# A two-layer hybrid mixer on one core: the prologue put in the order in which tokens and modulation weights arrive

## The chip, the core and the metric

The kernel runs on one NeuronCore of one Trainium2 chip. Five engines have queues of their own, each worked off in order: TensorE (PE; its weight loads are listed apart as PEld), VectorE (DVE), ScalarE (ACT), GpSimd (POOL) and SyncE (SP, which here issues most of the DMA transfers). The metric is the time of one execution in microseconds, the median of several runs.

## What is computed

Two layers of a mixer on 1024 latent tokens and 256 context tokens, all of width 1024. The change touches only the beginning of the first layer:

```python
shift, scale, gate = jnp.split(jax.nn.silu(c) @ w_mod + b_mod, 3, axis=-1)
shift_c, scale_c, gate_c = jnp.split(jax.nn.silu(c_ctx) @ w_mod + b_mod, 3, axis=-1)
h = rms_norm(x, norm_g) * (1 + scale[:, None]) + shift[:, None]
hc = rms_norm(ctx, norm_g) * (1 + scale_c) + shift_c
...
p = h @ w_in
```

After that come Fourier mixing, pooling, attention, a gated output product and a residual, twice.

## The kernel before

A token tile is 128 tokens by 1024 channels. Tiles 0 to 3 are group 0, tiles 4 to 7 group 1 (both latent), tiles 8 and 9 group 2 (context). The channels are cut into eight slices k of 128. For each slice and group, here called a block (k, g), the prologue makes the transposed, modulated tokens `H[k]`, split into a high and a low part of 32-bit matmul operands, and multiplies them at once with the first gate chunk of `w_in`:

- a token tile is loaded by an SP transfer of 512 KB (`x_load`, L256); ScalarE squares it in two halves and sums (L266); GpSimd turns the sum into the factor 1/rms (L267 to L269, the last a power); VectorE scales the tile with it (`norm`, L575);
- TensorE transposes slice k of the tiles of the group into one PSUM bank (L280); VectorE (L286) or ScalarE (L284) applies scale and shift; ScalarE rounds to the high part (L287); GpSimd (groups 0 and 1) or VectorE (group 2) subtracts to get the low part (L289);
- TensorE does the block's gate product (`gk`, L340): six matmuls, two output halves times high by high, low by high and high by low, summed over k in PSUM.

Scale and shift come from `w_mod`. A modulation product q (0 to 3) reads four transfers of 512 KB (`mod0_load`, L148), and yields scale and shift of slices 2q and 2q+1. Products 0 to 2 are eight 32-bit matmuls on TensorE each (`mod0_mm`, L157), after which `mod0_fin` copies the row (VectorE, L162), transposes it back (TensorE, L166) and adds bias and gain (`mod_finish`, VectorE, L136 to L141). Product 3 is done by VectorE in 32 multiply-adds (L176, L178), and 16 small matmuls sum it (`mod0_sum`, L187).

SP issues in this order: twelve modulation transfers (products 0 to 2), two halves of the gate chunk, ten token tiles, four modulation transfers (product 3), the next weight chunk. The order of the blocks is written out by hand in `items`: slices 0 to 5 of group 0, then of group 1, then of group 2, then slices 6 and 7 of all three groups. The list `at` says at which place the norm of a tile and the pieces of product 3 are put in. The gate product of a block stands three blocks behind its transposes. PSUM has eight banks here; the six gate sums hold six of them.

After the prologue `fourier_mix` puts eight small matmuls (L384) into the TensorE queue, and the next chunk's product follows (L340 from 92.42 us on).

Of the kernel before, what the change touches and what calls it, by code (L numbers as in the profile page):

```python
# [31 lines left out]
def build(tc, I, out):  # L32
# [127 lines left out]
    def mod0_fin(q, pm):  # L160
        row = E2()
        dve.tensor_copy(row[0:2, :], pm[0:2, :])  # L162
# [4 lines left out]
        mod_finish(0, 2 * q, psv[:, 0], psv[:, 1])  # L167

    def mod0_acc(ws, acc):
        for k in range(KT):  # L170
            for i in range(2):
                w = ws[k // 2][:, k % 2, i * 256:i * 256 + 256]
                for t in range(2):
                    a, sk = acc[:, 2 * i + t, :], sc[:, k, t:t + 1]
                    if k == 0:
                        dve.tensor_scalar(a, w, sk, None, MULT)  # L176
                    else:
                        dve.scalar_tensor_tensor(a, w, sk, a, MULT, ADD)  # L178
            yield

    def mod0_sum(q, acc):
        ps = PX()
        psv = ps[:, 0:8].rearrange("p (i c t) -> p i c t", i=2, c=2)
        for i in range(2):
            for ct in range(2):
                for t in range(2):
                    pe.matmul(psv[:, i, ct, t:t + 1], lhsT=acc[:, 2 * i + t, ct * 128:ct * 128 + 128],  # L187
                              rhs=ones[:, 0:1], start=True, stop=True)
        mod_finish(0, 2 * q, psv[:, 0], psv[:, 1])
# [83 lines left out]
    def h_block(l, k, g, xn, H, on_act=False):  # L273
        tiles = GROUPS[g]
        s = 1 if g == 2 else 0
        n = 128 * len(tiles)
        c0 = tiles[0] * 128
        ps = PX()
        for i, j in enumerate(tiles):
            pe.transpose(ps[:, i * 128:i * 128 + 128], xn[j][:, k * 128:k * 128 + 128], ident)  # L280
# [8 lines left out]
        eng.tensor_tensor(H[k][1][:, c0:c0 + n], hf[:, :n], H[k][0][:, c0:c0 + n].bitcast(F32), SUB)  # L289

# [241 lines left out]
    def layer(l, src, dst, carry):  # L532
# [27 lines left out]
        if full:  # L560
# [16 lines left out]
            def hb(k, g, on_act):  # L577
                newH(k)
                h_block(l, k, g, xn, H, on_act)

            def gk(k, *gs):
                for ct in range(2):
                    proj_T_k(psg[ct], H, W, ct, ntokA, k, gs)
# [768 lines left out]
```

## Time and profile before

| | us |
|---|---|
| median of 3 runs | 1451.82 (1447.77 to 1453.87) |
| the profiled execution | 1448.99 |
| its span (first to last instruction) | 1447.0 |
| first gate matmul (TensorE, L340) | 38.14 |
| first matmul behind the prologue (L384) | 90.42 |
| first matmul of the next chunk's product (L340) | 92.42 |

The page gives for each engine the busy time and its share of the span. A row in order of time gives the start and the length in us, engine, line and operation, output and inputs, shape and count of what was merged, and in brackets how long the engine had been idle before it and what ended that. A stage row gives start and end of a stretch, its length, the busy us (and the count of instructions) of PE, PEld, DVE, ACT and POOL in that order, then the mean clock granted to TensorE as a share of 2.4 GHz (0.50 is 1.2 GHz), the busy share of the DMA engines and GB/s.

### The profile page before, as it was taken

The numbers are of one execution on the slowest core, as the hardware profiler recorded it, in microseconds if no ns is written. First come the engines' busy times: TensorE is split into PE (matmuls) and PEld (weight loads), VectorE is DVE, ScalarE is ACT, GpSimd is POOL, SyncE is SP. The second block draws the span as 40 slices with busy tenths as digits, with TensorE's granted clock in tenths as the row PEclk, the third lists the DMA queues.
The fourth block names the chain that finished last, engine by engine and source line by source line (L and its number), as shares of the span: only waits on it lengthen the run. The fifth ranks groups of instructions, "written<-read, shape, count | busy, mean of one in ns | idle before, by whom it ended". The sixth has DMA issues, their size and how long they took to land.

```text
span 1447.0 us, 24063 instructions
## 1 busy us (share of the span) xinstructions
PE 1381.8 (95%) x9364; PEld 1240.6 (86%) x9364; DVE 979.2 (68%) x1553; ACT 567.6 (39%) x1230; POOL 775.9 (54%) x827
## 2 busy tenths in 40 slices
PE   7899999899999998999999899999999999999998
PEld 1688899779999987888888778988999998888887
DVE  2853366886895178798898654573464319989896
ACT  2632212101232265666665433121131227656663
POOL 2543222456785057667677842226887107766664
PEclk9899999999999999999999999999999999999999
DMA  9220242575123032112113321526412202111110
GB/s 354 101 90 32 85 149 91 187 266 166 60 88 117 1 103 81 66 45 74 45 45 112 104 66 38 205 80 213 148 44 85 78 22 67 45 45 45 59 59 30
DMA packets 65153, 137.07 MB, mean 95 GB/s; under 512 B 7312, under 2 KB 19728, under 8 KB 65040
## 3 DMA queue, kind: packets, MB, share of 16 engines
q1 hardware_dynamic: 49712, 108.82, 22.5%
q10 hardware_dynamic: 15328, 26.72, 5.3%
q8 instruction: 74, 1.21, 0.3%
q14 instruction: 39, 0.32, 0.1%
HBM read 105.63 MB, written 29.88 MB: 94 GB/s over the span
## 4 chain that ended last, share of the span: by engine, by line
PE 46%; DVE 21%; POOL 7%; issue 3%; ACT 2%; DMA 2%; ACTq 0%; POOLq 0%; SPq 0%; DVEq 0%
PE x L360 16%; DVE sm L923 6%; PE S L913 6%; PE x L1056 6%; PE x L993 5%; PE x L340 5%; PE x L753 3%; DVE e L1020 3%; PE x L977 2%; DVE t L952 1%; DVE t L980 1%; POOL e L759 1%; POOL sm L803 1%; DVE t L210 1%; PE x L892 1%
## 5 line engine op out<-in xcount | busy, mean ns | idle before, releaser
L360 PE MATMUL x<-wh,t 128*128 128x256 f32 x2432 | 445.9, 285 | 0.1
L360 PEld LDWEIGHTS x<-wh,t 128*128 128x128 f32 x2432 | 381.7, 192 | 1.8 <-issue 1.0
L360 PE MATMUL x<-wl,t 128*128 128x256 f32 x1216 | 344.7, 283 | 0.0
L923 DVE TENSOR_REDUCE sm<-S 128x1 f32<-128x1280 f32 (+1 forms) x132 | 194.8, 1476 | 72.2 <-PE S L913 72.0
L360 PEld LDWEIGHTS x<-wl,t 128*128 128x128 f32 x1216 | 233.7, 192 | 1.3 <-issue 1.2
L913 PE MATMUL S<-t,e 128*128 128x512 f32 (+1 forms) x768 | 180.9, 371 | 2.8 <-ACT e L899 1.4
L340 PE MATMUL x<-t,wh 128*128 128x512 f32 (+1 forms) x640 | 173.3, 381 | 8.8 <-DVE t L289 4.3
L938 ACT ACTIVATE t<-S,sm 128x1280 f32<-128x1280 f32 (+1 forms) x140 | 171.7, 1230 | 1.2 <-DVE sm L923 1.2
L993 PE MATMUL x<-t,t 128*128 128x128 f32 x1312 | 157.5, 275 | 3.3 <-DVE t L980 2.7
L993 PEld LDWEIGHTS x<-t,t 128*128 128x128 f32 x1312 | 153.7, 192 | 6.4 <-DVE t L980 2.9
L913 PEld LDWEIGHTS S<-t,e 128*128 128x128 f32 x768 | 126.3, 190 | 20.6 <-ACT t L938 2.0
L340 PEld LDWEIGHTS x<-t,wh 128*128 128x128 f32 x640 | 114.1, 192 | 31.6 <-POOL t L289 5.4
L318 POOL TENSOR_TENSOR wl<-st,wh 128x1024 fp32r<-128x1024 f32 x36 | 93.1, 2587 | 84.3 <-ACT wh L317 83.6
L961 POOL TENSOR_TENSOR t<-t,t 128x768 f32<-128x768 f32 (+1 forms) x64 | 116.2, 1816 | 5.3
L317 ACT ACTIVATE wh<-st 128x1024 fp32r<-128x1024 f32 x64 | 64.8, 1059 | 138.4 <-DMA xpart<-e 45.8
L977 PE MATMUL x<-ident,t 128*128 128x128 f32 x636 | 101.2, 274 | 5.7 <-DVE e L1059 4.1
L953 POOL TENSOR_SCALAR t<-t,sm 128x768 f32<-128x768 f32 x62 | 83.4, 1344 | 42.8 <-DVE sm L949 26.6
L753 PE MATMUL x<-wh,t 128*128 128x512 f32 x288 | 93.6, 404 | 8.5 <-DVE t L528 4.7
L1056 PE MATMUL x<-wh,e 128*128 128x512 f32 (+1 forms) x312 | 98.9, 384 | 2.6 <-ACT e L899 1.0
L340 PE MATMUL x<-t,wl 128*128 128x512 f32 (+1 forms) x320 | 100.2, 374 | 0.0
L210 DVE SCALAR_TENSOR_TENSOR t<-t,sc,t 128x512 f32<-128x512 f32 x98 | 90.8, 968 | 1.5 <-DMA t<-in_wmB_dram 1.1
L977 PEld LDWEIGHTS x<-ident,t 128*128 128x128 f32 x636 | 75.1, 141 | 15.9 <-DVE e L1059 4.5
(224 smaller groups left out, 2318.0 us busy)
## 6 DMA issues: line engine op xcount, KB each, us to landing
st<-in_w_in_dram SPq DMA_DIRECT2D x48, 512.0 KB, 4.0
t<-in_wmB_dram ACTq DMA_DIRECT2D x24, 512.0 KB, 5.4
xpart<-e ACTq DMA_DIRECT2D x36, 256.0 KB, 3.8
t<-xpart SPq DMA_DIRECT2D x18, 512.0 KB, 3.9
t<-in_wmS_dram SPq DMA_DIRECT2D x16, 512.0 KB, 8.5
st<-in_w_out_dram SPq DMA_DIRECT2D x16, 512.0 KB, 5.1
t<-in_x_dram SPq DMA_DIRECT2D x10, 512.0 KB, 10.3
e<-in_x_dram SPq DMA_DIRECT2D x20, 256.0 KB, 4.5
```

The source lines that it names most:

```text
L210: dve.scalar_tensor_tensor(a, w, sk, a, MULT, ADD)
L318: lo_eng[hf].tensor_tensor(lo[:, sl, :], st, hi[:, sl, :].bitcast(F32), SUB)
L340: pe.matmul(p[:, :m], lhsT=W[wi][:, k, ct * 128:ct * 128 + 128], rhs=H[k][hi][:, c0:c0 + m], start=(n == 0), stop=(n == 3 * KT - 1))
L360: pe.matmul(bank[:, i * 256:i * 256 + 256], lhsT=H[k][hi][:, j * 128:j * 128 + 128], rhs=W[wi][:, k, :], start=(n == 0), stop=(n == 3 * KT ...
L753: pe.matmul(ps, lhsT=zr[k][zi][:, j * 128:j * 128 + 128], rhs=W[wi][:, k, :], start=(n == 0), stop=(n == 11))
L913: pe.matmul(S[:, i * nk + c:i * nk + c + n], lhsT=s["qT"][i][:, m * 2 + f, :], rhs=kT[2 * h + m][:, k0 + c:k0 + c + n], start=(f == 0), st ...
L923: dve.tensor_reduce(nb, S[:, :nh * nk].rearrange("p (h k) -> p h k", h=nh), AX.X, ALU.min)
L938: act.activation(p[:, sl], S[:, sl], AF.Exp, bias=nb[:, i:i + 1], scale=-1.0, accum_out=ls[:, i:i + 1])
L961: pool.tensor_tensor(p[0][:, cut:end], p[0][:, cut:end], p[1][:, cut:end], ADD)
L977: pe.transpose(ps[:, i * 128:i * 128 + 128], s["p"][0][:, (t0 + i) * 128:(t0 + i + 1) * 128], ident)
L993: pe.matmul(o[:, i * 128:i * 128 + 128], lhsT=s["PT"][:, i * nkt + t, :], rhs=vv[h][:, kt0 + t, :], start=(t == 0), stop=(t == nkt - 1))
L1056: pe.matmul(ps[:, :m], lhsT=zz[:, k, :], rhs=Wa[hf][wi][:, k, w0:w0 + m], start=(n == 0), stop=(n == 11))
```

## The change

SP now loads the gate chunk first, then tiles 0 to 3, modulation products 0 and 1, tiles 4 to 7, product 2, tiles 8 and 9, product 3, the next chunk. All four modulation products are matmuls on TensorE; they stand as entries 0 to 3 in `items`, among the blocks. `mod0_acc` and `mod0_sum` are gone, and the row's copy is now in `mod0_mm`. Of the factor 1/rms VectorE does the two small steps and GpSimd only the power. `h_block` is cut in two, `h_trans` (transposes) and `h_split` (the rest); at a modulation product the transposes of the next block are issued ahead of it. The six gate sums get their banks when they are first used. The line numbers of the same steps change: L157 to L155, L162 to L157, L166 to L164, L280 to L252, L284/L286 to L262/L264, L287 to L265, L289 to L267, L340 to L321, L575 to L561, L266 to L554, L269 to L557.

```diff
-    def mod0_mm(ws, half_way=None):
+    def mod0_mm(ws):
         ps = PX()
         for k in range(KT):
-            if k == KT // 2 and half_way:
-                half_way()
             pe.matmul(ps[0:2, :], lhsT=sc[:, k, :], rhs=ws[k // 2][:, k % 2, :], start=(k == 0), stop=(k == KT - 1))
-        return ps
...
         row = E2()
-        dve.tensor_copy(row[0:2, :], pm[0:2, :])
+        dve.tensor_copy(row[0:2, :], ps[0:2, :])
+        return row
...
-    def mod0_acc(ws, acc):
...
-    def mod0_sum(q, acc):
...
             def rms(*js):
                 for j in js:
                     rx[j] = SM(1)
-                    for _ in x_rms(xn[j], rx[j]):
-                        pass
+                    ss = SM(2)
+                    for hf in range(2):
+                        sq = E2()
+                        act.activation(sq, xn[j][:, hf * 512:hf * 512 + 512], AF.Square, accum_out=ss[:, hf:hf + 1])
+                    dve.tensor_tensor(rx[j], ss[:, 0:1], ss[:, 1:2], ADD)
+                    dve.tensor_scalar(rx[j], rx[j], 1.0 / D, EPS, MULT, ADD)
+                    pool.tensor_tensor(rx[j], rx[j], mhalf[:, 0:1], ALU.pow)
...
-            wm = [mod0_load(q) for q in range(3)]
             w_dma()
-            x_in(0, 1, 2, 3, 4, 5, 6, 7, 8, 9)
-            ms = [mod0_mm(wm[0])]
-            ms.append(mod0_mm(wm[1], lambda: mod0_fin(0, ms[0])))
-            ms.append(mod0_mm(wm[2], lambda: mod0_fin(1, ms[1])))
+            x_in(0, 1, 2, 3)
+            wm = [mod0_load(q) for q in range(2)]
+            x_in(4, 5, 6, 7)
+            wm.append(mod0_load(2))
+            x_in(8, 9)
+            wm.append(mod0_load(3))
             w_split()
             W = wready.pop(0)
...
-            items = [(k, g) for g in (0, 1, 2) for k in range(6)] + [(k, g) for k in (6, 7) for g in (0, 1, 2)]
+            w_dma()
+            for j in range(4):
+                rms(j)
+                norm(j)
+            items = [0, (0, 0), (1, 0), 1, (2, 0), (3, 0)] + [(k, 1) for k in range(4)] + [2]
+            items += [(k, g) for k in (4, 5) for g in (0, 1)] + [(k, 2) for k in range(6)] + [3]
+            items += [(k, g) for k in (6, 7) for g in (0, 1, 2)]
             at = {n: [] for n in range(len(items))}
...
+            for n, j in ((3, 4), (3, 5), (4, 6), (5, 7), (11, 8), (12, 9)):
+                at[n] += [lambda j=j: rms(j), lambda j=j: norm(j)]
+            late, ahead = [], {}
...
+            for n, it in enumerate(items):
+                if isinstance(it, int):
+                    look(n + 1)
+                    row = mod0_mm(wm[it])
                     for f in at[n]:
                         f()
-                    hb(*items[n], 6 <= n < 17)
...
+                    if late:
+                        gk(*late.pop(0))
+                    mod0_fin(it, row)
+                    continue
+                for f in at[n]:
+                    f()
+                newH(it[0])
+                look(n)
+                h_split(l, *it, ahead[it], H, n % 2 == 1 and n > 10)
+                late.append(it)
+                if len(late) > 3:
+                    gk(*late.pop(0))
...
                 if n == 22:
                     w_split()
                     w_dma()
+            for it in late:
+                gk(*it)
```

How the order of instructions changes is seen at three places. The first is VectorE where tiles 4 to 7 are scaled. Before, the scaling of a tile (L575, `t_21` to `t_24` are tiles 4 to 7) stands between the scale-and-shift steps (L286) of group 0:

```order
L286 TENSOR_SCALAR e_71_302<-x_297,scaleT_99,shiftT_97 128x512
L575 TENSOR_SCALAR t_21_158<-t_21_158,sm_286 128x1024
L286 TENSOR_SCALAR e_85_335<-x_330,scaleT_99,shiftT_97 128x512
L575 TENSOR_SCALAR t_22_160<-t_22_160,sm_319 128x1024
L286 TENSOR_SCALAR e_93_356<-x_351,scaleT_99,shiftT_97 128x512
L575 TENSOR_SCALAR t_23_162<-t_23_162,sm_340 128x1024
L286 TENSOR_SCALAR e_101_377<-x_372,scaleT_99,shiftT_97 128x512
L575 TENSOR_SCALAR t_24_164<-t_24_164,sm_361 128x1024
```

In the changed kernel, on VectorE, tiles 4 to 7 are `t_17` to `t_20`, and `x_276` is the sum of modulation product 1:

```order
L157 COPY e_65_285<-x_276 2x512
L555 TENSOR_TENSOR sm_287<-sm_288 128x1
L556 TENSOR_SCALAR sm_287<-sm_287 128x1
L561 TENSOR_SCALAR t_17_150<-t_17_150,sm_287 128x1024
L555 TENSOR_TENSOR sm_297<-sm_298 128x1
L556 TENSOR_SCALAR sm_297<-sm_297 128x1
L561 TENSOR_SCALAR t_18_152<-t_18_152,sm_297 128x1024
L136 TENSOR_TENSOR shiftT_97<-x_315,bmodT 128x4
```

The scaling of the four tiles now stands behind the copy of product 1's row.

The second place is ScalarE, where tiles 4 and 5 (`t_21`, `t_22`) were squared; before, the two squares of a tile stood there one tile at a time among the high parts (L287) of group 0:

```order
L266 ACTIVATE e_66_288,sm_287<-t_21_158 128x512
L266 ACTIVATE e_67_290,sm_287<-t_21_158 128x512
L287 ACTIVATE t_68_295<-e_71_302 128x512
L266 ACTIVATE e_80_321,sm_320<-t_22_160 128x512
L266 ACTIVATE e_81_323,sm_320<-t_22_160 128x512
L287 ACTIVATE t_82_328<-e_85_335 128x512
```

In the changed kernel ScalarE has this where tiles 6 (`t_19`) and 7 (`t_20`) are squared; `t_82` is the high part of block (2, 0), made from `e_84`, which VectorE writes behind the scaling of tile 6:

```order
L554 ACTIVATE e_80_327,sm_326<-t_19_154 128x512
L554 ACTIVATE e_81_329,sm_326<-t_19_154 128x512
L265 ACTIVATE t_82_335<-e_84_337 128x512
L554 ACTIVATE e_87_343,sm_342<-t_20_156 128x512
L554 ACTIVATE e_88_345,sm_342<-t_20_156 128x512
L265 ACTIVATE t_89_351<-e_92_358 128x512
```

The squares of tile 7 moved behind the high part of block (2, 0), whose scale and shift come from modulation product 1.

The third place is TensorE ahead of the first transposes of group 1 (`x_442`); before, the end of the gate product of block (2, 0) stood directly in front of them:

```order
L340 MATMUL x_231<-t_90_349,wh_221 128x512
L340 MATMUL x_231<-t_91_350,wh_221 128x512
L340 MATMUL x_231<-t_90_349,wl_222 128x512
L280 MATMUL x_442<-ident,t_21_158 128x128
L280 MATMUL x_442<-ident,t_22_160 128x128
L280 MATMUL x_442<-ident,t_23_162 128x128
L280 MATMUL x_442<-ident,t_24_164 128x128
```

In the changed kernel TensorE has this behind modulation product 1; the first row transposes its row back, `x_353` takes the transposes of block (3, 0), `x_362` those of (0, 1), and the last rows begin the gate product of (1, 0):

```order
L164 MATMUL x_315<-ident,e_65_285 128x2 x4
L252 MATMUL x_353<-ident,t_5_126 128x128
L252 MATMUL x_353<-ident,t_6_128 128x128
L252 MATMUL x_353<-ident,t_7_130 128x128
L252 MATMUL x_353<-ident,t_8_132 128x128
L252 MATMUL x_362<-ident,t_17_150 128x128
L252 MATMUL x_362<-ident,t_18_152 128x128
L252 MATMUL x_362<-ident,t_19_154 128x128
L252 MATMUL x_362<-ident,t_20_156 128x128
L321 MATMUL x_307<-t_59_260,wh_178 128x512
L321 MATMUL x_307<-t_60_261,wh_178 128x512
```

The transposes of group 1 moved from behind three gate products of group 0 to a place behind one; those of (1, 0), (2, 0) and (3, 0) now stand behind them.

## Rows read from the trace of the kernel before

**Rows 1.** The page, part 1: busy us, share of the span, instructions
```profile
PE 1381.8 (95%) x9364; PEld 1240.6 (86%) x9364; DVE 979.2 (68%) x1553; ACT 567.6 (39%) x1230; POOL 775.9 (54%) x827
```

**Rows 2.** Stages: start:end length, busy by engine (instructions), PEclk, DMA, GB/s
```profile
29.70:33.26 3.56, 0.34 (x5) 0.32 (x5) 2.09 (x3) 2.55 (x8) 3.13 (x9) 1.00 1.03 412
33.26:40.70 7.44, 6.16 (x23) 4.84 (x22) 4.96 (x10) 3.60 (x10) 5.30 (x10) 0.56 1.04 393
...
64.75:69.05 4.30, 1.20 (x8) 1.00 (x8) 4.30 (x13) 1.66 (x4) 0.00 (x0) 0.91 0.15 36
69.05:78.35 9.30, 9.30 (x44) 9.17 (x44) 6.38 (x18) 1.32 (x3) 0.14 (x1) 0.50 0.49 147
...
92.42:200.00 107.58, 107.58 (x622) 94.06 (x623) 45.77 (x81) 27.91 (x52) 29.50 (x18) 1.00 0.20 72
```

**Rows 3.** Order of time, ScalarE: start, length, engine, line, operation, [idle before <-releaser]
```profile
23.20 1.06 ACT L317 ACTIVATE wh<-st 128x1024 fp32r<-128x1024 f32 x1 [20.25 <-DMA st<-in_w_in_dram]
...
25.75 0.63 ACT L266 ACTIVATE e<-t 128x512 f32<-128x512 f32 x1 [0.23 <-DMA t<-in_x_dram]
```

**Rows 4.** Order of time, TensorE, 0 to 40 us
```profile
5.93 12.61 PE L157 MATMUL x<-t,sc 128*2 128x512 f32 x24 [5.93 <-DMA t<-in_wmS_dram]
...
18.80 7.03 PE L157 MATMUL x<-t,sc 128*2 128x512 f32 x16
25.76 0.40 PE L166 MATMUL x<-ident,e 2*128 2x2 f32 x4
...
38.14 1.50 PE L340 MATMUL x<-t,wh 128*128 128x512 f32 x2
```

**Rows 5.** Order of time, TensorE, end of the prologue
```profile
90.42 1.06 PE L384 MATMUL x<-e 128*128 128x128 f32 x8
```

**Rows 6.** Order of time, TensorE, one block of a latent group
```profile
56.11 0.71 PE L340 MATMUL x<-t,wh 128*128 128x512 f32 x2
...
57.58 0.60 PE L280 MATMUL x<-ident,t 128*128 128x128 f32 x4
57.94 0.72 PE L340 MATMUL x<-t,wh 128*128 128x512 f32 x2
```

**Rows 7.** Order of time, TensorE, one block of the context group
```profile
79.25 0.38 PE L280 MATMUL x<-ident,t 128*128 128x128 f32 x2
79.38 0.48 PE L340 MATMUL x<-t,wh 128*128 128x256 f32 x2
...
80.18 0.38 PE L280 MATMUL x<-ident,t 128*128 128x128 f32 x2
```

**Rows 8.** Order of time, VectorE, first and last step of one mod_finish
```profile
18.91 0.16 DVE L136 TENSOR_TENSOR shiftT<-x,bmodT 128x4 f32<-128x4 f32 x1 [3.09 <-PE x L166]
...
19.38 0.16 DVE L141 TENSOR_TENSOR scaleT<-sm,ngT 128x4 f32<-128x4 f32 x1
```

**Rows 9.** Instructions of one line, 0 to 95 us: count, ns min/median/max
```profile
L162 DVE COPY e<-x x3: 672/679/679, 15.1 to 32.2; 2x512 f32<-2x512 f32 x3
...
L575 DVE TENSOR_SCALAR t<-t,sm x10: 739/754/1768, 30.1 to 51.4; 128x1024 f32<-128x1024 f32 x10
...
L266 ACT ACTIVATE e<-t x20: 612/616/632, 25.8 to 49.3; 128x512 f32<-128x512 f32 x20
...
L269 POOL TENSOR_TENSOR sm<-sm,mhalf x10: 548/550/937, 29.5 to 50.8; 128x1 f32<-128x1 f32 x10
...
L286 DVE TENSOR_SCALAR e<-x,scaleT,shiftT x13: 528/800/811, 36.0 to 87.1; 128x512 f32<-128x512 f32 x10, 128x256 f32<-128x256 f32 x3
...
L289 POOL TENSOR_TENSOR t<-e,t x16: 1272/1314/1748, 37.5 to 84.8; 128x512 fp32r<-128x512 f32 x16
```

**Rows 10.** Groups, 0 to 92.5 us: count, busy us, mean ns, idle
```profile
L287 ACT ACTIVATE t<-e 128x512 fp32r<-128x512 f32 x16 | 10.1, 629 | 16.0 <-DVE e L286 15.7
...
L318 POOL TENSOR_TENSOR wl<-st,wh 128x1024 fp32r<-128x1024 f32 x2 | 5.6, 2802 | 25.2 <-ACT wh L317 25.2
...
L317 ACT ACTIVATE wh<-st 128x1024 fp32r<-128x1024 f32 x4 | 4.1, 1049 | 20.5 <-DMA st<-in_w_in_dram 20.5
```

More of the change, by code (lines that the diff above doesn't have):

```diff
@@ L150, in mod0_load, with mod0_fin @@
         return ws
-    def mod0_mm(ws, half_way=None):
+    def mod0_mm(ws):
         ps = PX()
         for k in range(KT):
-            if k == KT // 2 and half_way:
-                half_way()
             pe.matmul(ps[0:2, :], lhsT=sc[:, k, :], rhs=ws[k // 2][:, k % 2, :], start=(k == 0), stop=(k == KT - 1))
-        return ps
-    def mod0_fin(q, pm):
         row = E2()
-        dve.tensor_copy(row[0:2, :], pm[0:2, :])
+        dve.tensor_copy(row[0:2, :], ps[0:2, :])
+        return row
+    def mod0_fin(q, row):
         ps = PX()
@@ L166, in mod0_fin @@
             pe.transpose(ps[:, 2 * i:2 * i + 2], row[0:2, i * 128:i * 128 + 128], ident[0:2, 0:2])
-        mod_finish(0, 2 * q, psv[:, 0], psv[:, 1])
-    def mod0_acc(ws, acc):
[L170 to L179, printed above, removed]
-    def mod0_sum(q, acc):
[L182 to L188, printed above, removed]
         mod_finish(0, 2 * q, psv[:, 0], psv[:, 1])
@@ L271, in build, with h_trans, h_split @@
     GROUPS = {0: (0, 1, 2, 3), 1: (4, 5, 6, 7), 2: (8, 9)}
-    def h_block(l, k, g, xn, H, on_act=False):
-        tiles = GROUPS[g]
-        s = 1 if g == 2 else 0
[L276 to L280, printed above, removed]
+    def h_trans(k, g, xn):
+        ps = PX()
+        for i, j in enumerate(GROUPS[g]):
+            pe.transpose(ps[:, i * 128:i * 128 + 128], xn[j][:, k * 128:k * 128 + 128], ident)
+        return ps
+    def h_split(l, k, g, ps, H, on_act=False):
+        s = 1 if g == 2 else 0
+        n = 128 * len(GROUPS[g])
+        c0 = GROUPS[g][0] * 128
         hf = E2()
@@ L289, in h_block @@
         eng.tensor_tensor(H[k][1][:, c0:c0 + n], hf[:, :n], H[k][0][:, c0:c0 + n].bitcast(F32), SUB)
+    def h_block(l, k, g, xn, H, on_act=False):
+        h_split(l, k, g, h_trans(k, g, xn), H, on_act)
     wsrc = []
@@ L575, in norm, with gk @@
                     dve.tensor_scalar(xn[j], xn[j], rx[j], None, MULT)
[L577 to L581, printed above, removed]
+            psg = [[None] * len(cols(ntokA)) for _ in range(2)]
+            def gk(k, g):
                 for ct in range(2):
-                    proj_T_k(psg[ct], H, W, ct, ntokA, k, gs)
-            wm = [mod0_load(q) for q in range(3)]
+                    if psg[ct][g] is None:
+                        psg[ct][g] = PX()
+                    proj_T_k(psg[ct], H, W, ct, ntokA, k, (g,))
@@ L601, in layer @@
-            for n in range(8, 16):
-                at[n] += [lambda: next(acc)]
-            at[18] += [lambda: mod0_sum(3, a3)]
-            for n in range(len(items) + 3):
-                if n < len(items):
+            w_dma()
[4 more added lines that the diff above has]
+            items += [(k, g) for k in (4, 5) for g in (0, 1)] + [(k, 2) for k in range(6)] + [3]
@@ new lines, in layer, with look @@
+            items += [(k, g) for k in (6, 7) for g in (0, 1, 2)]
+            at = {n: [] for n in range(len(items))}
+            for n, j in ((3, 4), (3, 5), (4, 6), (5, 7), (11, 8), (12, 9)):
+                at[n] += [lambda j=j: rms(j), lambda j=j: norm(j)]
+            late, ahead = [], {}
+            def look(n):
+                if n < len(items) and items[n] not in ahead and not isinstance(items[n], int):
+                    ahead[items[n]] = h_trans(*items[n], xn)
+            for n, it in enumerate(items):
+                if isinstance(it, int):
+                    look(n + 1)
+                    row = mod0_mm(wm[it])
```

12 lines of the change are left out of this document (removed).

## The prediction

> **What bounds the kernel now.** I read the page's engine line first: TensorE is busy for 95% of the span [rows 1]. That is an average, so the stage table comes next. From 92.42 us on TensorE has no gap for over 100 us [rows 2]; whatever the prologue gains or loses is handed on to the end in full. The prologue is where TensorE is not full, and it can be read as three parts. Up to 29.70 us TensorE does the 24 matmuls of modulation products 0 to 2 (two passes each, 48 rows of the trace) while the transfers come in; this work is free, since the tokens come later. Then it stands for most of 29.70 to 33.26 us, waiting for normed tokens, and its granted clock has a mean of 0.56 of 2.4 GHz in 33.26 to 40.70 us [rows 2]. The first gate matmul runs at 38.14 us [rows 4]. A second stand lies in 64.75 to 69.05 us (1.20 us busy of 4.30), and for the next 9.30 us the clock is at 0.50, its lower level of 1.2 GHz [rows 2]. The prologue ends, for my purpose, at 90.42 us, where the first matmul behind it runs [rows 5]. I ask where that point lies in the changed kernel.
>
> **Prices.** A modulation product on TensorE: 16 passes from 18.80 to 25.76 us, 6.96 us; transposing its row back: to the next row, about 0.34 us. The very first 24 passes took 12.61 us instead of 10.44, so starting cold costs 2.2 us [rows 4]. A block of a latent group: 1.47 us of gate matmuls (56.11 to 57.58) and 0.36 us of transposes (to 57.94) [rows 6]. A context block: 0.80 us (79.38 to 80.18) and 0.13 us [rows 7]. VectorE: row copy 0.68, scaling a tile 0.75, scale and shift of a block 0.80 [rows 9]; `mod_finish` 0.63 (18.91 to 19.54), each small step about 0.2 [rows 8]. ScalarE: a half-tile square 0.62 [rows 9], a high part 0.63, half a weight split 1.05 [rows 10]. GpSimd: the power 0.55, a low part 1.31 [rows 9], half a weight split 2.8 [rows 10].
>
> **The change, part by part.**
>
> *Arrival.* The first transfer of 512 KB was there at 5.93 us [rows 4], the fifteenth (tile 0) at 25.75 [rows 3]: 1.42 us apart. The total is the same 30 transfers, so by place in the new order tiles 0 to 3 arrive at 8.8 to 13.0 us, product 0 is complete at 18.7, product 1 at 24.4, tiles 4 to 7 by 30.0, product 2 at 35.7, tile 9 at 38.6, product 3 at 44.3. The tokens come 17 us earlier than before. The second chunk's two transfers are still the last of the thirty. The tables for the Fourier step are issued behind the context blocks as before and are needed only behind the prologue; I price them at nothing, and if that cover were gone they would cost about one transfer spacing each, 1.4 us. The gate split on ScalarE, VectorE and GpSimd moves to 6 to 11 us, where they had nothing to do, and costs nothing; if it held up tile 0's squares, 2 us.
>
> *Tiles 0 to 3.* VectorE now does two small steps (0.4), waits for the power (0.55), and scales (0.75): with hand-overs 1.8 us a tile, one after the other, since VectorE's queue stands at the wait. Tile 0's squares end near 10.0, so its scaling near 11.8 and tile 3's at 17.2. Their transposes stand ahead of product 0 on TensorE. Product 0 so starts at 17.4, not at 5.93: time in which TensorE had free work before is now empty. It takes 6.96 + 2.2 and ends at 26.6. Copy, transposing back and eight transposes: product 1 runs from 28.6 to 35.6, the gate product of (0, 0) to 37.1, the transposes of (3, 0) to 37.8.
>
> *Tiles 4 to 7, the term that decides.* The transposes of (0, 1) stand next on TensorE, ahead of the gate product of (1, 0), whose operands are ready. They need tiles 4 to 7 scaled, and on VectorE that stands behind the copy of product 1's row, which can't run before 35.7. From there: copy to 36.4; tile 4 to 38.2; tile 5 to 40.0; `mod_finish` to 40.7; tile 6 to 42.5; scale and shift of (2, 0) to 43.3. Only then can ScalarE make the high part of (2, 0) (43.9), and only behind it square tile 7 (45.2); two small steps, the power and the scaling bring it to 47.0, with hand-overs 47.3. Queued behind the wait are all later gate products; TensorE stands from 37.8 to 47.3 but for three transposes, 9.2 us. In the trace of before such a wait has no match. Its nearest row is a scaling, with 0.739 us at best and 1.768 at worst [rows 9]; the worst case on all four tiles adds 4 us, the best takes nothing away worth counting.
>
> *What is left at 47.3 us.* 15 latent gate products, 22.05 us; 8 context ones, 6.40; 11 sets of four transposes, 3.96; 8 of two, 1.04; products 2 and 3, 13.92; two rows back, 0.68. Sum 48.05, so 95.4 us if TensorE never waits again. Product 3 is the addition here (6.96 us); what it replaces on VectorE, and the 16 small matmuls, were beside or inside the stretch of the low clock.
>
> *Waits after that.* Behind product 2, ScalarE makes block (4, 0) first and then squares tile 9, VectorE scales tiles 8 and 9, and only then comes scale and shift of (4, 1): counted from the end F of product 2 its high part is ready at F + 8.3 and its low part at F + 9.7, while TensorE has work of its own to F + 7.4. That is 2 us. Behind product 3 (its end E) the transposes of (6, 1) wait for the bank of the row (0.7); those of (7, 0) for a bank that ScalarE empties behind both halves of the weight split (ready E + 6.2, TensorE there at E + 4.0: 2.2); the low part of (6, 1) stands behind GpSimd's half of that split, and (7, 1) ends on a low part: about 1 more. Together 6; between 4 and 9, the upper end with the low parts and splits at their longest.
>
> *Low clock.* In the trace a stand of 3.2 us in 3.56 and one of 3.1 in 4.30 were each followed by a stretch at low clock, 6.16 us busy at 0.56 (an estimate of the loss: 6.16 x 0.44 = 2.7 us) and 9.30 us at 0.50 (loss 4.65) [rows 2]. A stand of 9.2 us is far longer than either; it costs one such stretch. The two places of waits above may bring one or two. I take two stretches, one of each size, 7.4 us; none is the lower end, three long ones (14) the upper.
>
> **Sum.** 95.4 + 6 + 7.4 = 108.8, against 90.42: 18.4 us later, and all of it is kept. The profiled execution lasted 1448.99 us, its span 1447.0; the median of the runs is 1451.82, so 2.8 above it. The profile after should show about 1467, the median about 1470.
>
> **The rivals.**
>
> *A. As forecast*, one or two low stretches: +12 to +28 us, 1464 to 1480.
>
> *B. The clock holds.* The stand of 9.2 us is there, yet no low stretch follows: 95.4 + 6 = 101.4, or 99.4 with the waits at 4: +9 to +11, 1461 to 1463. Against it: both stands in the trace were followed by one.
>
> *C. The clock never holds.* Three long stretches, waits at 9, scalings at their worst: 95.4 + 4 + 9 + 14 = 122.4, +32, 1484. For it: the 16 one-column matmuls and transposes of before stayed at 0.50 right through 69.05 to 78.35 [rows 2]. The Trainium skill, "TensorE: Matmul & The Clock Gate", section "HAM oscillation — how this bites in real kernels", tells of a matmul kernel whose every burst behind a transfer wait starts at half rate again; by that rule this change, which puts matmul bursts between waits, would end at C's 1484. The trace agrees as far as two of two long stands lowered the clock.
>
> *D. Not slower: the interleaving works.* If tiles 4 to 7 are scaled while product 1 runs, TensorE never waits after 28.6 us: three products (20.88), 16 latent and 8 context gate products (23.52 + 6.40), 13 and 8 sets of transposes (4.68 + 1.04), rows back (1.02), 57.5 in all, so 86.1: 4.3 us earlier, 1447.5. It decides at 37.8 us: tile 7 must be scaled by then. For it: tile 7 arrives at 30.0. Against it: the order on VectorE and ScalarE, which does not ask when a tile arrived. The Trainium skill, "Perfetto Trace Analysis", section "Optimization Strategy", says that a kernel whose bound changes from one stage to the next may gain by interleaving those stages; by it D's 1447.5 would be the time. In before the two stages are already laid over each other up to 29.70 us, where transfers and modulation matmuls run together.
>
> *E. Faster by more*: also product 0 ahead of the transposes, from 14 us on: another 3.5 us, 1444. The order shows transposes first.
>
> *F. The lead isn't there.* Except at the modulation products, the transposes of a block still stand right ahead of its own scale and shift, as before; this is in the sum already and has no price of its own.
>
> **How the numbers follow.** A 0.68, B 0.11, C 0.11, D 0.07, E 0.03. The forecast is A's 1470. The range of 8 in 10 reaches from B's lower end nearly to C: 1460 to 1482. About 0.5% (7.3 us) is what a measurement of this kernel can tell from no change: A, B and C lie beyond it on the slow side (0.90), D within it (0.07), E on the border of the fast side (0.03).
>
> **What would show it.** Right: in the profile after, TensorE stands some 9 us ahead of the transposes of (0, 1), released by the scaling on VectorE; product 1 ends near 36 us; the first gate matmul is a little earlier than 38.14, the first matmul behind the prologue is near 109. Wrong: tile 7 scaled before 40 us (D), a clock of 1.00 right behind the stand (B), or a gap in 92 to 260 us that takes up the delay.

## The result, and the profile after

The changed kernel takes 1463.91 us (median; 1462.52 to 1466.80), against 1452.78 for the kernel before on the same chip: a ratio of 1.0086, 95% interval 1.0057 to 1.0115. It is slower, by more than the 0.5% that was named as the bound. The forecast was 1470 with a range of 1460 to 1482.

| us | before | after |
|---|---|---|
| the profiled execution | 1448.99 | 1462.52 |
| its span | 1447.0 | 1460.7 |
| first gate matmul | 38.14 | 35.16 |
| first matmul behind the prologue | 90.42 | 103.52 |
| first matmul of the next chunk | 92.42 | 105.52 |
| from there to the end | 1354.6 | 1355.2 |

So 13.1 of the 13.7 us of span are lost inside the prologue, and in these two executions nothing behind it takes them up or adds to them. The page's first line of after, which answers [rows 1], shows none of this: the share of TensorE is 95% again.

```profile
PE 1382.9 (95%) x9368; PEld 1234.7 (85%) x9368; DVE 961.7 (66%) x1545; ACT 565.5 (39%) x1227; POOL 768.0 (53%) x807
```

The stages of after (columns as in [rows 2]: stretch and length, busy us of PE, PEld, DVE, ACT, POOL, then PEclk, DMA share, GB/s):

```profile
0.00:29.70 29.70, 12.98 (x36) 3.64 (x37) 9.22 (x24) 9.84 (x23) 4.94 (x10) 1.00 0.94 341
29.70:37.90 8.20, 8.20 (x28) 2.86 (x26) 1.88 (x6) 4.12 (x13) 2.86 (x3) 1.00 1.05 395
37.90:46.00 8.10, 0.94 (x4) 0.36 (x4) 4.08 (x13) 1.85 (x5) 2.92 (x4) 0.68 0.81 308
46.00:50.90 4.90, 4.90 (x14) 3.95 (x15) 2.16 (x3) 1.43 (x3) 2.50 (x2) 0.50 0.01 3
...
71.50:76.00 4.50, 3.62 (x17) 2.74 (x18) 1.77 (x3) 2.65 (x5) 4.16 (x4) 1.00 0.34 86
...
88.00:94.00 6.00, 3.52 (x30) 3.11 (x29) 3.69 (x8) 3.42 (x5) 2.12 (x2) 1.00 0.00 0
94.00:104.00 10.00, 8.95 (x51) 7.26 (x50) 2.72 (x4) 3.62 (x7) 5.81 (x4) 1.00 0.31 105
105.52:200.00 94.48, 94.48 (x542) 82.83 (x543) 43.14 (x78) 24.67 (x47) 27.11 (x17) 1.00 0.22 74
```

TensorE stands for 7.2 of the 8.1 us from 37.9 to 46.0, then runs for 4.9 us at 0.50, 1.2 GHz. After that the clock stays at 1.00 through every later wait of the prologue. TensorE in order of time shows the same places, with what it waited for in brackets (answers to [rows 4, 5]):

```profile
17.78 8.29 PE L155 MATMUL x<-t,sc 128*2 128x512 f32 x16
...
28.20 7.03 PE L155 MATMUL x<-t,sc 128*2 128x512 f32 x16
35.16 0.73 PE L321 MATMUL x<-t,wh 128*128 128x512 f32 x2
...
39.34 0.33 PE L252 MATMUL x<-ident,t 128*128 128x128 f32 x1 [1.35 <-DVE t L561]
41.56 0.48 PE L252 MATMUL x<-ident,t 128*128 128x128 f32 x1 [1.89 <-DVE t L561]
45.96 0.47 PE L252 MATMUL x<-ident,t 128*128 128x128 f32 x1 [3.93 <-DVE t L561]
...
93.79 0.66 PE L252 MATMUL x<-ident,t 128*128 128x128 f32 x4 [2.07 <-ACT e L262]
...
103.52 1.06 PE L365 MATMUL x<-e 128*128 128x128 f32 x8
```

Why tile 7 is late stands in the queues of VectorE and ScalarE. VectorE of after, 35 to 46 us:

```profile
35.27 0.68 DVE L157 COPY e<-x 2x512 f32<-2x512 f32 x1 [5.78 <-PE x L155]
...
36.86 0.75 DVE L561 TENSOR_SCALAR t<-t,sm 128x1024 f32<-128x1024 f32 x1 [0.66 <-POOL sm L557]
...
44.14 0.16 DVE L555 TENSOR_TENSOR sm<-sm 128x1 f32<-128x1 f32 x1 [1.92 <-ACT e L554]
...
45.15 0.75 DVE L561 TENSOR_SCALAR t<-t,sm 128x1024 f32<-128x1024 f32 x1 [0.66 <-POOL sm L557]
```

ScalarE of after:

```profile
33.11 0.61 ACT L554 ACTIVATE e<-t 128x512 f32<-128x512 f32 x1
...
42.26 0.63 ACT L265 ACTIVATE t<-e 128x512 fp32r<-128x512 f32 x1 [8.44 <-DVE e L264]
42.79 0.61 ACT L554 ACTIVATE e<-t 128x512 f32<-128x512 f32 x1
```

VectorE was idle for 5.78 us up to 35.27, waiting for the row of product 1, while the squares of tiles 4 to 6 were done (the last at 33.8). ScalarE was idle for 8.44 us ahead of the high part of (2, 0), with tile 7's squares queued behind it. Both engines had time; their order did not let them use it.

### The profile page after: what moved, and what is told of

It is laid out like the page before. It is cut to its first block, busy times and chain, and to the rows that moved or that the text cites. A ratio compares the mean times of both kernels' runs of the same rounds, so it can differ in the third digit from the quotient of the medians.

```text
span 1460.7 us, 24039 instructions
## 1 busy us (share of the span) xinstructions
PE 1382.9 (95%) x9368; PEld 1234.7 (85%) x9368; DVE 961.7 (66%) x1545; ACT 565.5 (39%) x1227; POOL 768.0 (53%) x807
## 4 chain that ended last, share of the span: by engine, by line
PE 46%; DVE 20%; POOL 6%; issue 3%; DMA 3%; ACT 2%; ACTq 0%; SPq 0%; POOLq 0%; DVEq 0%
PE x L341 16%; PE S L914 6%; PE x L1057 6%; DVE sm L924 6%; PE x L994 5%; PE x L321 5%; PE x L754 3%; DVE e L1021 3%; PE x L978 2%; DVE t L953 1%; DVE t L981 1%; POOL sm L804 1%; PE x L893 1%; POOL wl L299 1%; POOL e L760 1%
## 5 line engine op out<-in xcount | busy, mean ns | idle before, releaser
L321 PE MATMUL x<-t,wh 128*128 128x512 f32 (+1 forms) x640 | 170.8, 378 | 5.3 <-POOL t L267 3.5
L321 PEld LDWEIGHTS x<-t,wh 128*128 128x128 f32 x640 | 112.7, 190 | 29.5 <-POOL t L267 5.4
L299 POOL TENSOR_TENSOR wl<-st,wh 128x1024 fp32r<-128x1024 f32 x36 | 92.5, 2569 | 67.7 <-ACT wh L298 63.7
L954 POOL TENSOR_SCALAR t<-t,sm 128x768 f32<-128x768 f32 x62 | 83.7, 1350 | 42.5 <-DVE sm L950 28.6
L321 PE MATMUL x<-t,wl 128*128 128x512 f32 (+1 forms) x320 | 99.7, 372 | 0.0
```

The source lines that it names most:

```text
L299: lo_eng[hf].tensor_tensor(lo[:, sl, :], st, hi[:, sl, :].bitcast(F32), SUB)
L321: pe.matmul(p[:, :m], lhsT=W[wi][:, k, ct * 128:ct * 128 + 128], rhs=H[k][hi][:, c0:c0 + m], start=(n == 0), stop=(n == 3 * KT - 1))
```

## The experiments

**Theory (queue):** the loss is the stand before 46.0 and the half clock behind it, because the scaling of tiles 4 to 7 stands behind product 1's row copy (VectorE) and behind a high part (ScalarE). **Rivals:** product 3's 6.96 us on TensorE (product theory); the first 12 to 17 us, in which TensorE now has no work (start theory).

All twelve runs; "ends" is the first matmul behind the prologue in the profiled execution, the ratio is to the kernel before on the same chip:

| run | ends, us | ratio | 95% interval |
|---|---|---|---|
| before | 90.42 | 1 | |
| after | 103.52 | 1.0086 | 1.0057 to 1.0115 |
| norm_ahead | 96.11 | 1.0056 | 1.0042 to 1.0070 |
| squares_early | 99.91 | 1.0083 | 1.0069 to 1.0098 |
| p2_in_gap | 93.42 | 1.0025 | 1.0015 to 1.0035 |
| fill_gap | 102.62 | 1.0083 | 1.0067 to 1.0100 |
| p3_vector | 106.86 | 1.0125 | 1.0111 to 1.0139 |
| p0_first | 105.94 | 1.0122 | 1.0103 to 1.0140 |
| combined | 91.84 | 1.0018 | 1.0009 to 1.0027 |
| combined_w | 93.00 | 1.0031 | 1.0017 to 1.0046 |
| before_p3 | 89.41 | 1.0003 | 0.9992 to 1.0014 |
| before_p3_copy | 90.27 | 0.9997 | 0.9985 to 1.0009 |
| before_rms | 87.55 | 0.9993 | 0.9982 to 1.0004 |
| before_three | 92.09 | 1.0012 | 1.0001 to 1.0024 |

### The stand: three ways to take it away

```diff
-            for n, j in ((3, 4), (3, 5), (4, 6), (5, 7), (11, 8), (12, 9)):
+            for n, j in ((3, 4), (3, 5), (3, 6), (3, 7), (11, 8), (12, 9)):
```

This alone is squares_early. In norm_ahead the row's copy moves out of `mod0_mm` as well:

```diff
...
+    def mod0_row(ps):
         row = E2()
         dve.tensor_copy(row[0:2, :], ps[0:2, :])
...
-                    row = mod0_mm(wm[it])
+                    pm = mod0_mm(wm[it])
                     for f in at[n]:
                         f()
+                    row = mod0_row(pm)
```

And p2_in_gap puts entry 2 of `items` behind (3, 0), with (0, 1)'s transposes behind it.

> The changed kernel with one move: the squares and the scaling of tiles 4 to 7 are all written ahead of the row copy of product 1, so on VectorE they no longer stand behind it. Queue theory (TensorE's 7.2 us of standing between 37.9 and 46.0, and the low clock up to 50.9 that follows it, come from the order of VectorE and ScalarE): tile 7 is scaled at about 37, its transposes follow at 38.6 instead of 46.0, standing falls from 7.2 to about 2 us, the stretch at half clock (a loss of 2.4) is gone; 7 to 9.5 us less than the changed kernel's 1463.9, so 1454.5 to 1457. Rival (the time is lost for good at the start of TensorE or in product 3, and what is won at 46 is waited for again at product 2 or behind it): within 3 us of 1463.9.

> The changed kernel with only ScalarE's part of that move: the squares of tiles 6 and 7 are written at product 1's place, ahead of the scale-shift and high part of block (2,0), but all four tiles' small steps and scaling still stand behind product 1's row copy on VectorE. Queue theory: tiles 4 to 7 are scaled one after the other from 36.86, each 1.68 later (small steps, GpSimd's power, scaling), so tile 7 at about 41.9 instead of 45.15: 3 to 4 us less, 1460 to 1461; the half clock stays in part. If the row copy did not matter and the squares were all of it: 7 us or more less, 1457 or below. If neither: 1463.9.

> The changed kernel with VectorE's and ScalarE's order left as it is, but with product 2 issued on TensorE behind the transposes of (3,0), where TensorE stands, instead of behind (3,1). Its weights were issued by 25 and took 10.5 us. Queue theory: the scaling of tile 7 stays at about 45, and 6.96 us of product 2 lie in the stand; TensorE's clock stays at full speed, so 7 + 2.4 less, 1454 to 1457, less whatever product 2's own row copy adds on VectorE (0.7). Rival (the start and product 3 are the price, a gap filled here opens again behind tile 7): within 3 us of 1463.9.

TensorE in norm_ahead, then its VectorE (L167, L255 and L564 are L164, L252 and L561 of after, L160 is the row copy; 37.62 is the scaling of tile 7):

```profile
39.01 0.41 PE L167 MATMUL x<-ident,e 2*128 2x2 f32 x4 [2.47 <-DVE e L160]
39.35 1.09 PE L255 MATMUL x<-ident,t 128*128 128x128 f32 x8
```

```profile
37.62 0.75 DVE L564 TENSOR_SCALAR t<-t,sm 128x1024 f32<-128x1024 f32 x1 [0.66 <-POOL sm L560]
38.29 0.67 DVE L160 COPY e<-x 2x512 f32<-2x512 f32 x1
```

The stand of 7.2 us is down to 2.47, no half clock follows, and the prologue ends 7.4 us earlier: inside the 7 to 9.5 expected. The time gains less: the median is 1458.26, where 1454.5 to 1457 was expected, and the ratio falls by 0.30%, 4.4 us; the intervals of the two overlap, so the time alone doesn't settle it. The profiled execution shows where a part went: its span is only 3.3 us shorter than after's, and in 465 to 470 us it has half clock (0.50) behind a wait of 2.64 us. After has the same wait, at 472.24, and keeps 1.00 behind it. In squares_early the transposes of tile 7 come at 42.4 instead of 46.0 and the prologue ends 3.6 earlier, as expected; but its median is 1463.38, not 1460 to 1461, and its ratio can't be told from after's. By the profiles the two moves are worth about the same: 3.6 us for the squares and 3.8 more for the row copy, 2.4 of these the half clock that squares_early still has. The row copy was not moved alone.

In p2_in_gap VectorE and ScalarE are as late as in after (tile 7 is scaled from 45.34, in after from 45.15), but TensorE has product 2 to do meanwhile:

```profile
37.86 7.03 PE L155 MATMUL x<-t,sc 128*2 128x512 f32 x16
```

```profile
45.34 0.75 DVE L561 TENSOR_SCALAR t<-t,sm 128x1024 f32<-128x1024 f32 x1 [0.66 <-POOL sm L557]
```

Stages of p2_in_gap and, below, of squares_early:

```profile
37.80:45.00 7.20, 7.20 (x19) 1.46 (x18) 3.46 (x14) 1.85 (x5) 2.62 (x4) 1.00 0.84 319
45.00:50.00 5.00, 4.03 (x24) 3.17 (x25) 4.09 (x9) 0.82 (x2) 1.58 (x2) 1.00 0.02 5
```

```profile
42.50:47.40 4.90, 4.90 (x15) 3.92 (x16) 3.38 (x6) 2.15 (x4) 2.96 (x3) 0.50 0.29 115
```

It ends 10.1 us earlier than after and has a ratio of 1.0025: 0.6% of the time back, as expected (7 + 2.4 us are 0.65%). One reordered entry gives back most of the loss. This run shows that most of the loss is the stand with the half clock behind it; that the order on VectorE and ScalarE makes the stand is shown by norm_ahead and squares_early. What is left, 0.25%, or 3.0 us of the prologue, is not taken apart by a run of its own.

### The half clock by itself

```diff
                 newH(it[0])
+                if n == 6:
+                    pf = PX()
+                    for k in range(KT):
+                        pe.matmul(pf[0:2, :], lhsT=sc[:, k, :], rhs=wm[1][k // 2][:, k % 2, :], start=(k == 0), stop=(k == KT - 1))
                 look(n)
```

> The changed kernel with sixteen matmuls that do nothing needed (product 1 once more, its result unread) issued on TensorE ahead of the transposes of (0,1), where it stands from 37.9 to 46.0. They are 6.96 us, so the stand is filled and nothing else is moved; this prices the half clock from 46.0 to 50.9 by itself. If the clock is set by the stand, the stretch runs at full speed: 4.9 us at half become 2.45, the prologue ends at 101.1 instead of 103.5, the time is 2.4 lower. If the half clock comes from something else (the work of the blocks (0,1) to (3,1) themselves): 103.5 and no change. If the low clock cost the 4 to 5 us that the prediction's two stretches would be worth each: below 100.

Stages of fill_gap, then TensorE at the two short waits that follow product 2:

```profile
46.00:51.00 5.00, 5.00 (x27) 4.15 (x27) 2.85 (x4) 2.17 (x4) 3.69 (x3) 1.00 0.01 3
71.20:75.00 3.80, 3.80 (x12) 2.81 (x12) 2.29 (x3) 0.96 (x3) 2.09 (x3) 0.55 0.66 180
```

```profile
69.07 0.49 PE L321 MATMUL x<-t,wh 128*128 128x512 f32 x1 [0.84 <-ACT t L265]
70.43 0.50 PE L321 MATMUL x<-t,wh 128*128 128x512 f32 x1 [0.86 <-POOL t L267]
```

Filling the stand did keep the clock at 1.00 behind it, so the stand was the cause. But the end moved by 0.9 us, not 2.4: another stretch at half clock came behind the two short waits, at 0.55 for 3.8 us (a loss of 3.8 x 0.45 = 1.7). After has the same two waits (0.83 and 0.86, at 71.52 and 72.88) and stayed at 1.00 there:

```profile
71.52 0.49 PE L321 MATMUL x<-t,wh 128*128 128x512 f32 x1 [0.83 <-ACT t L265]
72.88 0.50 PE L321 MATMUL x<-t,wh 128*128 128x512 f32 x1 [0.86 <-POOL t L267]
```

The price of 2.45 us holds for the stretch; it can't simply be added to a sum, because the next stretch may come instead.

### Product 3

```diff
...
+            a3 = T5([128, 4, 256])
+            acc = mod0_acc(wm[3], a3)
+            for n in range(12, 20):
+                at[n] += [lambda: next(acc)]
...
+                if it == 3:
+                    mod0_sum(3, a3)
+                    look(n + 1)
+                    continue
```

> The changed kernel with product 3 summed on VectorE in eight steps over blocks (5,1) to (5,2) and added up by sixteen small matmuls, as in the kernel before. Product theory (the price is product 3's 6.96 us on TensorE with its copy wait of 0.8): less 7.8, plus 16 small matmuls at 0.21 to 0.34, so 2.5 to 4.5 us less, 1459.5 to 1461.5; if product 3 were the whole of the loss, 1453. Queue theory: product 3 is worth this much and no more, and the stand before 46 stays as it is, 7.2 us; if VectorE's 32 steps delay the blocks of the context tiles, nothing is left of the gain, 1463.

The edit also puts `mod0_acc` and `mod0_sum` back as they were. All three numbers were wrong: with product 3 back on VectorE the prologue of the changed kernel ends 3.3 us later. Its TensorE, its VectorE (four of the multiply-adds), its GpSimd subtraction (L289), and below them the subtraction of after (L267), the last two as count and ns min/median/max:

```profile
76.47 0.80 PE L343 MATMUL x<-t,wh 128*128 128x512 f32 x1 [3.12 <-POOL t L289]
...
88.62 3.42 PE L185 MATMUL x<-ones,t 128*128 128x1 f32 x16 [0.26 <-ACT t L287]
```

```profile
75.93 3.99 DVE L176 SCALAR_TENSOR_TENSOR t<-t,sc,t 128x256 f32<-128x256 f32 x4
```

```profile
L289 POOL TENSOR_TENSOR t<-e,t x6: 1279/1452/3542, 67.4 to 99.2; 128x512 fp32r<-128x512 f32 x6
```

```profile
L267 POOL TENSOR_TENSOR t<-e,t x16: 1260/1282/1447, 29.5 to 100.1; 128x512 fp32r<-128x512 f32 x16
```

VectorE's multiply-adds stand in the way of the blocks beside them, one low part on GpSimd beside them takes 3.54 us instead of 1.28, and half clock follows (76.5 to 82.0 at 0.50). The Trainium skill, "SBUF — State Buffer", section "Who interferes with whom", says that a VectorE instruction with two SBUF inputs contends with a GpSimd instruction that reads SBUF; the multiply-add reads two. The trace agrees with 3.54 against 1.28. In the next overlap it was VectorE that lost: the two low parts right behind took about 1.46 each, and the four multiply-adds beside them 3.99 us, up to 1.50 for one against a median of 0.48.

The same part done alone on the kernel before:

```diff
-            a3 = T5([128, 4, 256])
...
-            for n in range(8, 16):
-                at[n] += [lambda: next(acc)]
-            at[18] += [lambda: mod0_sum(3, a3)]
+            at[17] += [lambda: ms.append(mod0_mm(w3))]
+            at[18] += [lambda: mod0_fin(3, ms[3])]
...
-                    acc = mod0_acc(w3, a3)
```

> The kernel before with one part of the change alone: product 3 on TensorE, its sixteen matmuls issued ahead of block (5,2) and its row copy behind, VectorE's 32 steps and the sixteen small matmuls gone. Product theory as the run on the changed kernel left it (VectorE's steps cost the context blocks more than product 3 costs TensorE): TensorE gains 7.0 + 0.4 us of work, loses 3.4 of small matmuls, 3.1 of standing (64.75 to 69.05) and about 3 of the 9.3 us at half clock that are not the small matmuls; the prologue ends about 2 us earlier, 88.3 instead of 90.4, ratio 0.998 to 0.999. If the half clock stays (the stand at 87.5 to 89.7 or another causes it): 91, ratio 1.000 to 1.001. If product 3 on TensorE is a price as its 7 us read: 94 or more, ratio 1.003.

The prologue ends 1.0 us earlier, but the last waits now fall so that half clock begins at its end (stage of before_p3, where the kernel before had 1.00):

```profile
89.00:95.00 6.00, 5.46 (x19) 4.51 (x19) 3.31 (x9) 4.42 (x15) 1.07 (x4) 0.51 0.26 96
```

A ratio of 1.0003: product 3 on TensorE is neither a price nor a gain in the kernel before, and in the changed kernel VectorE's way costs more. The product theory falls.

### The start

```diff
+            wm = [mod0_load(0)]
             x_in(0, 1, 2, 3)
-            wm = [mod0_load(q) for q in range(2)]
+            wm.append(mod0_load(1))
...
+            mod0_fin(0, mod0_mm(wm[0]))
             for j in range(4):
                 rms(j)
...
+                if n == 0:
+                    look(1)
+                    continue
```

> The changed kernel with product 0's weights loaded ahead of tiles 0 to 3 and product 0 done first, so TensorE starts at about 7 instead of 12.2; nothing else. Start theory (the first 12 us that TensorE stands are part of the price): 2 MB more ahead of the tiles, at the rate of this stretch some 5 us, so tile 3's transposes at about 22.5, product 1 at 22.9 instead of 28.2; row copy and tile 7's scaling 5 us earlier, at 40 instead of 45.2, and the prologue ends 5.3 us earlier, 98.2; time 1458 to 1459. Queue theory alone: the stand before tile 7 stays about as long (6 to 7 us), only shifted, which is the same number, so this run tells the start from no effect at all: if tiles 4 to 7 set the pace by their arrival, 1 to 2 us less.

The prologue ends 2.4 us later than after's. TensorE and VectorE of p0_first:

```profile
8.64 9.44 PE L155 MATMUL x<-t,sc 128*2 128x512 f32 x16 [8.64 <-DMA t<-in_wmS_dram]
...
26.70 2.18 PE L252 MATMUL x<-ident,t 128*128 128x128 f32 x9 [1.20 <-DVE t L561]
28.81 7.90 PE L155 MATMUL x<-t,sc 128*2 128x512 f32 x16
```

```profile
18.12 0.68 DVE L157 COPY e<-x 2x512 f32<-2x512 f32 x1 [10.11 <-PE x L155]
...
19.85 0.15 DVE L555 TENSOR_TENSOR sm<-sm 128x1 f32<-128x1 f32 x1
```

The experiment built the same trap once more: tile 0's small steps (19.85) stand on VectorE behind product 0's row copy (18.12), though its squares began at 15.02. Product 1 starts at 28.81, no earlier than the 28.20 of after. Half clock comes in as well: between product 0 and product 1 TensorE mostly stands, the granted clock is 0.54 in 20 to 25 us and 0.50 in 25 to 30, and product 1 takes 7.90 us instead of 7.03. So this run does not tell whether an earlier start would help; it shows that loading weights first doesn't, while the row copy stands ahead of the tiles.

### All together, and the other parts alone

> The changed kernel with three moves at once: product 0 first (as in p0_first), the squares of tiles 4 to 7 ahead of block (2,0) (as in squares_early), and product 2 issued behind the transposes of (3,0) (as in p2_in_gap). If the three prices add up: product 1 from 22.9 to 29.9, product 2 from about 32 to 39, block (0,1)'s transposes at about 41.5 instead of 47.8 of p2_in_gap, no stretch at half clock, the prologue ends at 87 to 88 against 90.4 of the kernel before: ratio 0.997 to 0.999 to it. Rival (the weights of product 2, 5.5 us later than the order of TensorE wants them, are waited for, or tile 7 again): ends at 91 to 93, ratio 1.000 to 1.002.

> As combined, and the next weights are split three blocks later, so ScalarE's two copies (1.99 us) and VectorE's subtraction (1.46) no longer stand ahead of block (6,1), where TensorE waited 2.07. If that wait is just won: 2 us less than combined, 85.5, ratio 0.996 to 0.998. Rival (the split weights are wanted right behind the last block, and are late): the wait reappears before the next chunk, no difference to combined or 1 to 2 us more.

The edits of combined are those of p0_first, squares_early and p2_in_gap together; combined_w splits the next weights at n == 25 instead of 22. Combined ends at 91.84, the rival's number but not by the rival's mechanism: product 2 runs at 37.46 and the transposes of (0, 1) at 46.35, neither with a wait for weights or for tile 7. Instead product 1 starts at 27.53 for the reasons just told (the granted clock is 0.65 in 25 to 30 us), and behind the weight split half clock comes in, which after did not have there. By its time combined can't be told from p2_in_gap alone. TensorE and a stage of combined:

```profile
37.46 7.03 PE L155 MATMUL x<-t,sc 128*2 128x512 f32 x16
...
82.12 0.66 PE L252 MATMUL x<-ident,t 128*128 128x128 f32 x4 [2.08 <-ACT e L262]
```

```profile
82.90:86.50 3.60, 3.60 (x13) 2.89 (x12) 2.04 (x2) 0.98 (x3) 2.70 (x2) 0.53 0.69 221
```

In combined_w that wait is 0.2 us, but TensorE then stands 1.05 us for a high part and 1.55 for a low part, where combined has no wait: it was moved, not won.

```profile
87.58 0.50 PE L321 MATMUL x<-t,wh 128*128 128x512 f32 x1 [1.05 <-ACT t L265]
89.63 0.58 PE L321 MATMUL x<-t,wh 128*128 128x512 f32 x1 [1.55 <-POOL t L267]
```

The last three runs are parts of the change on the kernel before:

```diff
-            at[0] += [lambda: rms(0, 1, 2, 3), lambda: norm(0, 1), lambda: mod0_fin(2, ms[2]), lambda: norm(2, 3)]
+            at[0] += [lambda: rms(0, 1, 2, 3), lambda: mod0_fin(2, ms[2]), lambda: norm(0, 1, 2, 3)]
```

This, with product 3 on TensorE, is before_p3_copy. In before_rms the body of `rms` is after's, all else before's; before_three has all three.

> As before_p3, and product 2's row copy written on VectorE ahead of the scaling of tiles 0 and 1, where TensorE stood 3.23 us for it. Queue theory (a row copy and the scaling of tiles that meet on VectorE: which stands first decides): the transposes of the copied row start at about 30.4 instead of 32.9, but the tiles' transposes still wait for tile 3's scaling at 35.4, so the end of the prologue moves by less than 1 us, 87.5 to 88.3; only if the half clock from 33.3 to 40.7 goes with the stand is there more, 2 to 3 us. Rival: tiles 0 and 1 are scaled 0.7 later and everything behind them too: 0.7 more than before_p3.

> The kernel before with another part of the change alone: of the three small steps ahead of each tile's scaling two on VectorE and only the power on GpSimd. Queue theory: VectorE is asked for the small steps of tiles 0 to 3 ahead of the first scaling, so it waits for the squares of tile 3 (30.4), and the first scaling is at about 31.9 instead of 30.05; the four then follow without a pause, tile 3 is scaled at about 35 as before; GpSimd has some 10 us less to do up to 55. End of the prologue within 1 us of 90.4, ratio 0.9995 to 1.0005. If GpSimd's small steps hold back the low parts of the blocks (the waits of 1.5 us for it): 1 to 1.5 us less. If VectorE's waiting for squares holds back the blocks: 2 us more.

> The kernel before with everything of the change that does not touch the order of arrival: product 3 on TensorE as in before_p3, product 2's row copy ahead of the scaling as in before_p3_copy, two of the three small steps on VectorE as in before_rms. If the price of the change is the order of arrival alone, these three together cost nothing: ratio 0.997 to 1.000, the prologue ends between 86.5 and 90.3. If the parts add up as the single profiles read (0.1 and 2.9 us less): 87.4, ratio 0.998. If they get in one another's way (VectorE now has the row copy behind the small steps that wait for tile 3's squares): 91 to 92, ratio 1.001.

The first two can't be told from the kernel before. The third is 0.12% slower; its VectorE shows the order named last in the expectation, the small steps waiting for tile 3's squares with the row copy behind them:

```profile
30.83 0.16 DVE L574 TENSOR_TENSOR sm<-sm 128x1 f32<-128x1 f32 x1 [0.86 <-ACT e L573]
...
31.10 0.67 DVE L162 COPY e<-x 2x512 f32<-2x512 f32 x1
```

That wait is only 0.86 us, and the copied row is transposed back at 31.82, earlier than in the kernel before (32.92): what costs the 0.12% is not shown. So the parts that leave the order of arrival alone cost 0.01 to 0.24% together. By difference, the larger part of the 0.86% belongs to the new order, with the steps interleaved as they are. No version here is measurably faster than the kernel before; the best on the new order, combined, is still 0.09 to 0.27% slower.

## Why the prediction was right, and where a term was off

- **Arrival, tiles 0 to 3, products 0 and 1.** Forecast: product 0 at 17.4, product 1 from 28.6 to 35.6, gate product of (0, 0) to 37.1, TensorE free at 37.8. Measured: 17.78, 28.20 to 35.16, 36.7, 38.0. Right within 0.5 us.
- **The term that decides.** Forecast: tile 7 scaled at 47.3, TensorE standing but for three transposes. Measured: scaled by 45.9 and transposed at 45.96; the stands in between sum to 7.17 us, not 9.2. Same chain in the same order: row copy, tiles 4 and 5, `mod_finish`, tile 6, (2, 0), its high part, tile 7's squares. It was 1.3 us too long: product 1 ended 0.4 us earlier, the four tiles took 1.67 us each rather than 1.8 (0.5 in all), and the rest is hand-overs.
- **Work left.** Forecast 48.05. From 45.96 to 103.52 are 57.6 us, less 5.2 of waits and 2.45 of half clock: 49.9, so 1.9 too little. About 0.7 of this lies where TensorE goes from a product to transposes and back, which the rows of one even block didn't show; most of the rest lies at the waits, most of which cost 0.2 to 0.3 us more than the idle time in their brackets: the matmul at 71.52 holds TensorE for 0.49 ahead of the next wait, one in an even block for 0.24.
- **Waits after that.** Forecast 6 (4 to 9). Measured 0.83 + 0.86 behind product 2, 0.41 + 2.07 + 0.82 + 0.23 behind product 3: 5.2. The wait of 2.2 for the bank that ScalarE empties behind the weight split was 2.07.
- **Low clock: the term that was mis-sized.** Forecast 7.4 for two stretches. There was one, 4.9 us at 0.50, worth 2.45. The places named for a second one had their waits and kept the clock. This is 4.9 of the 5.3 us between 108.8 and 103.5. That the error is nearly the clock's alone is in part luck: the other terms, 1.3 and 0.8 too much and 1.9 too little, nearly cancel.
- **The rivals.** B (the clock holds) fails at the stand and holds everywhere behind it. By the profile the 13.1 us lost lie just inside A's +12 to +28, with one stretch of the smaller size; the median lies between B's 1463 and A's 1464. For C the page "TensorE: Matmul & The Clock Gate" of the Trainium skill, section "HAM oscillation — how this bites in real kernels", was cited, by which every burst behind a transfer wait starts at half rate; of the three places with waits (ahead of tile 7, behind product 2, behind product 3) the trace shows one where it did. D's condition, tile 7 scaled by 37.8, was not met in after, and even norm_ahead, which comes near it (tile 7 scaled from 37.62, the row copy behind it), ends at 96.1 and not at 86.1: the row copy waits instead, and the tail waits remain.
- **A reading of the kernel before that was off.** The prediction has TensorE stand from 29.70 to 33.26 us for normed tokens. What ended that stand was the row copy of product 2, which on VectorE stood behind the scaling of tiles 0 and 1. The kernel before so has a small case of the same trap; moving that copy forward (before_p3_copy) gained nothing that the times show. TensorE of before:

```profile
32.92 0.41 PE L166 MATMUL x<-ident,e 2*128 2x2 f32 x4 [3.23 <-DVE e L162]
```

Why the new order doesn't win even when repaired is argued, not shown by a run of its own: up to 29.70 us TensorE was busy for 23.76 us before, 12.98 in after and 14.59 in combined (there partly at half clock). Weights go from the transfer straight to TensorE; a tile must first pass ScalarE, VectorE, GpSimd and VectorE, in after one tile every 1.67 us. Loading tokens first puts the slow path where TensorE had work that needed no one else.

## What to carry over

When two streams are interleaved for the engine that bounds, look at the in-order queues of its helpers: a small step that waits for that engine (a row copy of 0.68 us) holds up everything behind it, and the engine then waits for itself. Put independent work (here a whole product, 7 us) into the place where it would wait. Loading first what the bounding engine can use without help is argued above and not shown: p0_first, which tried it, kept the trap and was slower. Price a loss of clock from the stretch it covers, but give it a wide range: it moves when anything ahead of it moves.

## What the runs showed of the hardware that was not expected

- **Equal waits, unequal clock.** Waits of 0.83 and 0.86 us left the clock at 1.00 in after (71.5 to 76.0); 0.84 and 0.86 us in the same two instructions were followed by 0.55 in fill_gap (71.2 to 75.0). One of 2.07 us left it at 1.00 in after (94 to 104), one of 2.08 in combined led to 0.53; far behind the prologue one of 2.64 did the same in after (1.00) and in norm_ahead (0.50). In the first two pairs TensorE's rows right ahead are the same; what made the difference is not shown. A single profile so carries a few us of luck: before_rms ends its prologue 2.9 us earlier than before, but its ratio says 0.07%.
- **GpSimd beside VectorE.** A subtraction of 128x512 took 3.54 us at worst beside VectorE's multiply-adds in p3_vector, 1.45 at worst in after, which has none; a multiply-add beside the next subtractions took up to 1.50 us against a median of 0.48.
